# A hybrid two-layer encoder on one core: a reordered beginning, routing and end, and experts of 64 slots in one stationary operand

## The chip, the cores and the metric

The kernel runs on one core of a Trainium2 chip. The metric is the device time of one execution in microseconds (us). Five engines work side by side, each through its own list of instructions in order: TensorE (PE, matmuls), VectorE (DVE), ScalarE (ACT), GpSimd (POOL) and SyncE (SP, which here issues the transfers). Semaphores make one wait for another.

## What is computed

256 tokens of width 1024 pass two layers. Each layer takes a modulated norm of x, a mixer (gated linear attention, differential attention and gated delta net, merged by gates), a residual, a second modulated norm, a feed-forward part and a residual. The feed-forward part of layer 0 is dense (width 2816), that of layer 1 is a mixture of eight experts of width 3584, of which each token takes the best two:

```python
mod = jnp.einsum('bd,lde->lbe', jax.nn.silu(c), adaln_w) + adaln_b[:, None, :]
for layer in range(DEPTH):
    sh1, sc1, g1, sh2, sc2, g2 = jnp.split(mod[layer][:, None, :], 6, axis=-1)
    h = rmsnorm(x, norm_w[layer, 0]) * (1.0 + sc1) + sh1
    y = hybrid_mixer(h, ...)
    x = x + g1 * rmsnorm(y, norm_w[layer, 1])
    h = rmsnorm(x, norm_w[layer, 2]) * (1.0 + sc2) + sh2
    y = swiglu(h, ...) if layer % 2 == 0 else moe_swiglu(h, ...)
    x = x + g2 * rmsnorm(y, norm_w[layer, 3])
def swiglu(h, w1, w3, w2):
    return (jax.nn.silu(h @ w1) * (h @ w3)) @ w2
def moe_swiglu(h, router_w, w1, w3, w2):
    top_val, top_idx = lax.top_k(t @ router_w, TOP_K)
    combine = einsum(softmax(top_val), one_hot(top_idx, N_EXPERTS))
    for e in range(N_EXPERTS):
        out = out + combine[:, e:e + 1] * swiglu(t, w1[e], w3[e], w2[e])
```

## The kernel before

All weights are fp32 and are read once, in tiles of 128x1024 (two blocks of 128 input rows by 512 columns, 512 KB). For every tile SP starts a DMA into a ring of `raw` slots (line 286); ACT casts its high part `wh` (L319); DVE subtracts it from the tile and keeps the low part `wl` (L320, the *split* below). An activation is held in the same way as a high and a low part, and PE makes three products: high by high, high by low, low by high. The tiles come in a planned order: `load_ahead` issues transfers, `take` gives the next split tile, and casts and splits are issued some four tiles ahead of the matmuls that use them. `Side` and `pump` weave smaller work (a generator that yields how many steps it wants to wait) between the tiles; inside `by_hand` the order of the program is the order of each engine.

The stages, by time in the profile: the beginning (to 55 us), mixer 0 (to about 350), the dense ffn (to 545), mixer 1 (to 870), routing (to 895), the experts (to 1840) and the end.

*Beginning.* `begin` loads x and sixteen `rawe` tiles of adaln_w for shift and scale. `sums` accumulates each tile either on PE (L509, against the column `scol`) or on DVE (L450, L452) into `acc`, which `end` then sums over partitions on PE. The first eight tiles give columns 0 to 511 of the modulation, and with them the first half of the projection `gv` (`mm_nat`, L400 to L403) runs; the late eight tiles give the other half. `gates_small` (L841) multiplies a small tile of w_in (`small`, L831 to L833), and `proj_T("nk")` (L439) follows.

*Transitions.* `transition` interleaves the residual `r` (squares L724, `yg` = y times the gain row L730, `rr` = the reciprocal root L692 and L693, `up` L737) with the next norm `n` (squares L639, `xn` L648, transposes `tr` L660, modulated columns `hf` L668 and L670, their high part `hi` L674 and low part `lo` L678) for token blocks 0 and 1. `down_proj` is the matmul group before it.

*Experts.* Routing sorts the experts by their count. The five biggest get 128 slots (*full*), the last three get 64 (*half*); a run-time branch at the end repeats the work with 128 slots for all if a half expert had more than 64 tokens. `gather` picks an expert's tokens by matmuls with one-hot matrices (L1884), eight blocks for the high part and eight for the low part, casts them to `gx` (L1887), and transposes the one-hots to `hT` (L1899). It runs for groups of experts (0), (1), (2, 3), (4, 5), (6, 7), each from block 4 of the expert before on. An expert has seven blocks of 512 hidden columns. A block takes four tiles of w1, four of w3 and, of the block before, four of w2. The up-projection is L1991 to L1993 (1 of 128 rows `gH`, `gL` each times a 128x512 piece). `gated` makes silu (ACT, L2001) and the multiply (DVE, L2002) at 128x512. `turned` transposes the product on PE (L1946) and keeps high and low part (`aTm`). `down` multiplies it (L1913, L1914 for half experts, L1916 to L1918 for full ones).

In a half expert, the one-hot stands twice side by side: rows 0 to 63 and rows 64 to 127 of the gathered tile are the same 64 tokens. The two halves of the transposed tile then hold the high and the low part of the same tokens, so that `down` needs two matmuls in place of three. The up-projection makes three with the tokens doubled.

After an expert's last block, `parted` keeps `ywH` and `ywL` (L1925, L1926) and `scatter` (L1938 to L1940) adds it to `acc` with the routing weight. `finish` applies the last residual.

## Time and profile before

| | us |
|---|---|
| median of three runs (1858.14 to 1862.54) | 1859.29 |
| the profiled execution | 1858.87 |
| its span, first to last instruction | 1857.0 |
| PE busy in the span | 1817.3 (98%) |
| DVE busy | 1591.7 (86%) |
| ACT busy | 1319.6 (71%) |
| POOL busy | 28.2 (2%) |
| DMA, mean over the span | 286 GB/s, 531 MB |

The busy times of engines overlap. PE is nearly always busy, so the chain that ended last is 73% PE; by its lines the three up-projection matmuls of the experts have 11% of the span each. DVE's largest group is L320 (893 splits, 1066.6 us), ACT's is L319 (893 casts, 927.5 us). The share over the whole span is a mean over stages, so the rows below go by stages.

### The profile page before, as it was taken

What the parts mean: (1) busy time and instruction counts of PE and PEld (TensorE: products, weight loads), DVE (VectorE), ACT (ScalarE), POOL (GpSimd) and SP (SyncE); (2) the same over time, 40 slices, a digit from 0 to 9 for tenths busy, and PEclk for the clock granted to TensorE, in tenths of its full rate; (3) what the DMA queues carried; (4) which work ended last, traced back from release to release, by engine and by line L of the source; (5) the groups of instructions that cost most, each with busy time, mean ns of one, the idle gap of its engine ahead of it and who ended that gap; (6) DMA issues with size and microseconds to landing.
All of it is one profiled execution on the core that took longest, in us unless ns stands there. A gap on an engine that the chain in (4) does not pass through costs nothing.

```text
span 1857.0 us, 33213 instructions
## 1 busy us (share of the span) xinstructions
PE 1817.3 (98%) x11988; PEld 1534.8 (83%) x11988; DVE 1591.7 (86%) x2034; ACT 1319.6 (71%) x1872; POOL 28.2 (2%) x54
## 2 busy tenths in 40 slices
PE   7999999999999999999999999999999999999997
PEld 6987888799978978888788888888888888878785
DVE  6887986788856888867898998999989999999998
ACT  3786476644456774774788788787787778888885
POOL 0000000000000000000000000000000000000000
PEclk9999999999999999999999999999999999999998
DMA  9545765699764547669899999999999999999993
GB/s 323 164 145 149 238 193 184 204 311 302 237 210 126 148 149 229 204 201 328 289 350 318 358 347 348 360 377 356 369 349 359 378 366 383 393 382 393 393 393 141
DMA packets 258027, 531.35 MB, mean 286 GB/s; under 512 B 22126, under 2 KB 45116, under 8 KB 257852
## 3 DMA queue, kind: packets, MB, share of 16 engines
q1 hardware_dynamic: 257500, 528.99, 82.0%
q8 instruction: 96, 1.57, 0.4%
q14 instruction: 79, 0.65, 0.1%
q0 software_dynamic: 192, 0.07, 0.0%
q10 hardware_dynamic: 160, 0.07, 0.0%
HBM read 528.02 MB, written 1.05 MB: 285 GB/s over the span
## 4 chain that ended last, share of the span: by engine, by line
PE 73%; DVE 3%; DMA 2%; ACT 1%; issue 1%; POOL 0%; DVEq 0%; ACTq 0%
PE mo L1992 11%; PE mo L1991 11%; PE mo L1993 11%; PE my L1916 3%; PE my L1917 3%; PE my L1918 3%; PE pt L439 3%; PE pt L440 3%; PE pt L441 3%; PE pn L400 3%; PE pn L403 3%; PE pn L401 2%; DVE wl L320 2%; PE my L1914 2%; PE my L1913 2%; PE maT L1946 1%
## 5 line engine op out<-in xcount | busy, mean ns | idle before, releaser
L320 DVE TENSOR_TENSOR wl<-raw,wh 128x1024 fp32r<-128x1024 f32 (+1 forms) x893 | 1066.6, 1220 | 142.4 <-ACT wh L319 112.9
L319 ACT CAST wh<-raw 128x1024 fp32r<-128x1024 f32 (+1 forms) x893 | 927.5, 1054 | 319.1 <-PE mo L1993 79.5
L1991 PE MATMUL mo<-wh,gx 128*128 128x512 f32 x896 | 355.7, 397 | 0.1
L1992 PE MATMUL mo<-wl,gx 128*128 128x512 f32 x896 | 350.4, 391 | 2.0 <-DVE wl L320 1.9
L1993 PE MATMUL mo<-wh,gx 128*128 128x512 f32 x896 | 349.8, 390 | 0.0
L1992 PEld LDWEIGHTS mo<-wl,gx 128*128 128x128 f32 x896 | 168.6, 188 | 38.8 <-DVE wl L320 5.6
L1993 PEld LDWEIGHTS mo<-wh,gx 128*128 128x128 f32 x896 | 168.2, 188 | 35.7 <-ACT gx L1887 0.4
L1991 PEld LDWEIGHTS mo<-wh,gx 128*128 128x128 f32 x896 | 168.4, 188 | 32.7 <-ACT gx L1887 0.5
L439 PE MATMUL pt<-xH,wh 128*128 128x256 f32 x576 | 166.4, 289 | 0.0
L440 PE MATMUL pt<-xH,wl 128*128 128x256 f32 x576 | 163.7, 284 | 0.0
L441 PE MATMUL pt<-xL,wh 128*128 128x256 f32 x576 | 163.6, 284 | 0.0
L400 PE MATMUL pn<-wh,xH 128*128 128x512 f32 x352 | 148.2, 421 | 0.0
L403 PE MATMUL pn<-wh,xL 128*128 128x512 f32 x352 | 138.1, 392 | 0.0
L401 PE MATMUL pn<-wl,xH 128*128 128x512 f32 x352 | 137.9, 392 | 0.2 <-issue 0.2
L440 PEld LDWEIGHTS pt<-xH,wl 128*128 128x128 f32 x576 | 111.3, 193 | 0.2
L439 PEld LDWEIGHTS pt<-xH,wh 128*128 128x128 f32 x576 | 111.2, 193 | 0.3
L441 PEld LDWEIGHTS pt<-xL,wh 128*128 128x128 f32 x576 | 111.2, 193 | 0.0
L1916 PE MATMUL my<-wh,aTm 128*128 128x512 f32 x280 | 109.1, 390 | 0.0
L1917 PE MATMUL my<-wl,aTm 128*128 128x512 f32 x280 | 109.0, 389 | 0.0
L1918 PE MATMUL my<-wh,aTm 128*128 128x512 f32 x280 | 108.9, 389 | 0.0
L400 PEld LDWEIGHTS pn<-wh,xH 128*128 128x128 f32 x352 | 66.2, 188 | 18.6 <-issue 7.4
L403 PEld LDWEIGHTS pn<-wh,xL 128*128 128x128 f32 x352 | 66.1, 188 | 14.8
(476 smaller groups left out, 2639.2 us busy)
## 6 DMA issues: line engine op xcount, KB each, us to landing
raw<-in_moe_w SPq DMA_DIRECT2D x672, 512.0 KB, 5.8
raw<-in_w_in SPq DMA_DIRECT2D x128, 512.0 KB, 4.0
raw<-in_ffn_w SPq DMA_DIRECT2D x66, 512.0 KB, 5.0
raw<-in_adaln_w SPq DMA_DIRECT2D x48, 512.0 KB, 4.1
rawa<-in_adaln_w SPq DMA_DIRECT2D x32, 512.0 KB, 6.3
raw<-in_w_branch SPq DMA_DIRECT2D x24, 512.0 KB, 4.7
rawe<-in_adaln_w SPq DMA_DIRECT2D x16, 512.0 KB, 7.9
raw<-in_w_out SPq DMA_DIRECT2D x16, 512.0 KB, 4.7
```

The costliest lines, as they stand in the source:

```text
L319: S.copy(H, r)
L320: low = lambda: tt(L, r, H, op=OP.subtract)
L400: mm(o, xH[:, tb, k, :], H, start=k == 0, stop=False)
L401: mm(o, xH[:, tb, k, :], L, start=False, stop=False)
L403: mm(o, xL[:, tb, k, :], H, start=False, stop=k == last)
L439: mm(d, H[:, cs], xH[:, :, k, :], start=k == 0 and c % 2 == 0, stop=False, skip_group_check=True)
L440: mm(d, L[:, cs], xH[:, :, k, :], start=False, stop=False, skip_group_check=True)
L441: mm(d, H[:, cs], xL[:, :, k, :], start=False, stop=k == KD - 1, skip_group_check=True)
L1916: mm(y[hf], aT[:, 0, k, :], H[:, c], start=first, stop=False)
L1991: mm(q, gH[:, k, :], H, start=k == 0, stop=False)
L1992: mm(q, gH[:, k, :], L, start=False, stop=False)
L1993: mm(q, gL[:, k, :], H, start=False, stop=k == KD - 1)
```

## The change

1. *Beginning.* The order of x, rows and adaln tiles in SP's queue changes; the `small` tile is loaded behind the last gv tiles and all of its matmuls come later; the late tiles that PE sums are numbers 4 and 5 instead of 0; `product` runs per token block; constants (`other_loads`) load later; two matmuls `keep_warm` stand around the first sums' end.
2. *Transitions and routing.* The second token block's squares come before the multiplies by the gain row; in `down_proj`'s last tiles block 1 makes its left half first; in routing, transposes take the place of warm matmuls.
3. *Half experts.* The tokens are gathered once, 64 wide, and one `gx` tile holds their high part in columns 0 to 63 and their low part in 64 to 127. The up-projection then makes two matmuls for three. Its result has two halves of partitions that must be added. `gated` only copies both results from PSUM (two ACT copies). `turned`, now after the second w1 tile of the next block, multiplies each 128x128 piece by `fold`, two identities of 64 on top of each other, which transposes and adds; then silu on ACT and multiply on DVE at 128x256, and the high (ACT) and low part (DVE) of the product. The one-hots are doubled by POOL (`twice`) for `hT`. Groups of the gather: (0), (1), (2, 3), (4), (5, 6, 7).
4. *End.* Token block 0's two multiplies `yg` run on POOL, ahead of the reciprocal roots, and block 1's come before the stores.

```diff
+    def keep_warm():
+
+        mm(ps("warm", [P, 512], "pw"), ident, x[:, 0, 0:512], start=True, stop=True)
+
@@ -542,12 +546,15 @@
             s0.add(v, k0, load(v, 0, k0), i in (1, 3))
             part(i)
         load_ahead([None] * 2)
-        order = [(1, 0), (1, 2), (1, 4), (1, 6), (0, 0), (0, 2), (0, 4), (0, 6)]
-        late = [load(v, 1, k0) for v, k0 in order[:2]]
-        load_ahead([None, None, "l4"])
-        late += [load(v, 1, k0) for v, k0 in order[2:]]
+        order = [(v, k0) for v in (1, 0) for k0 in range(0, KD, 2)]
+        late = [load(v, 1, k0) for v, k0 in order[:3]]
+        load_ahead([None] * 2)
+        late += [load(v, 1, k0) for v, k0 in order[3:]]
+        late = [(v, k0, r, i in (4, 5)) for i, ((v, k0), r) in enumerate(zip(order, late))]
         lows = []
+        keep_warm()
         s0.end()
+        keep_warm()
         issue_one()
         issue_one(lows)
         s0.bias()
@@ -562,33 +569,32 @@
         load_ahead([None] * 2)
         o = [ps("pn", [P, 512], "pw") for _ in range(2)]
-        def product(early, tb, i):
-            for k, H, L in early:
-                mm_nat(o[tb], k, H, L, xs, tb, KD - 1, (i,))
+        def product(early, tb):
+            for i in range(2):
+                for k, H, L in early:
+                    mm_nat(o[tb], k, H, L, xs, tb, KD - 1, (i,))
         s1 = sums(1)
-        late = [(v, k0, r, i == 0) for i, ((v, k0), r) in enumerate(zip(order, late))]
+        early = [p for _ in range(2) for p in take("gv", False)]
+        product(early, 0)
         s1.add(*late[0])
-        early = [p for _ in range(2) for p in take("gv", False)]
-        for tb in range(2):
-            for i in range(2):
-                product(early, tb, i)
+        s1.add(*late[1])
         issue_one()
-        s1.add(*late[1])
-        small = take("small", False)
-        osm = gates_small(xs, small[:4])
-        issue_one()
-        load_ahead([None] * 2)
-        other_loads()
+        product(early, 1)
         s1.add(*late[2])
-        issue_one()
+        issue_one(lows)
+        lows.pop()()
+        load_ahead([None])
         s1.add(*late[3])
-        s1.end(1)
         n.tr(0, 1, ("pg",))
         n.tr(1, 1, ("pl",))
+        s1.add(*late[4])
+        s1.add(*late[5])
+        s1.add(*late[6])
         onk = proj_T("nk", 512, xs, rows=2)
-        for i in range(4, 8):
-            s1.add(*late[i])
+        other_loads()
+        s1.end(1)
+        s1.add(*late[7])
         issue_one(lows)
...
         n.tr(0, 0)
         n.tr(0, 1)
         warm(fill)
+        r.sq(1, 0)
         r.yg(1, 0, grow)
-        r.sq(1, 0)
         then()
-        r.yg(1, 1, grow)
         r.sq(1, 1)
         r.rs(1)
+        r.yg(1, 1, grow)
...
         def by_block(n, between):
             ps_ = [p for _ in range(n) for p in take(name, False)]
             for tb in range(2):
-                for k, H, L in ps_:
-                    for hf in range(2):
-                        add_(k, H, L, tb, hf)
+                todo = [(p, hf) for p in ps_ for hf in range(2)]
+                for (k, H, L), hf in sorted(todo, key=lambda t: t[1]) if tb else todo:
+                    add_(k, H, L, tb, hf)
                 if between and tb == 0:
                     between()
@@ -1864,27 +1865,34 @@
                 slots, m, comb, half = tl("slb", [P, 2, NE], "gs"), m01, combk, ()
                 tt(slots, slot, first_slot[:, None, :].to_broadcast([P, 2, NE]), op=OP.subtract)
             nb = DE // 512
-            groups = deque(((0,), (1,), (2, 3), (4, 5), (6, 7)))
+            groups = deque(((0,), (1,), (2, 3), (4,), (5, 6, 7)) if half else ((0,), (1,), (2, 3), (4, 5), (6, 7)))
+            if half:
+
+                fold = abT[:, 0:64]
+                tt(fold, ident[:, 0:64], ident[:, 64:128], op=OP.add)
             def gather(es, every):
                 hot = hots.pop(0) if hots else one_hot(slots, m, es, half)
                 if es[0]:
-                    yield 16
-                n = len(es)
-                gs = [[tl("gx", [P, KD, P], "e4", F32R) for _ in range(2)] for _ in es]
+                    yield 10 if es[0] in half else 16
+                n, small = len(es), es[0] in half
+                width = 64 if small else P
+
+                gs = [[tl("gx", [P, KD, P], "e4", F32R) for _ in range(1 if small else 2)] for _ in es]
                 hT = [tl("hT", [P, 2, P], "l1", F32R) for _ in es]
                 for j, e in enumerate(es):
                     of[e] = gs[j], hT[j]
                 for k in range(0, KD, 2):
                     for part, src in enumerate((hH, hL)):
-                        o = ps("gx", [P, 2, n, P])
+                        o = ps("gx", [P, 2, n, width])
                         for i in range(2):
                             for tb in range(2):
                                 mm(o[:, i], src[:, tb, (k + i) * P:(k + i) * P + P], hot[tb],
                                    start=tb == 0, stop=tb == 1)
                         for j in range(n):
-                            S.copy(gs[j][part][:, k:k + 2, :], o[:, :, j, :])
+                            g = gs[j][0][:, :, part * 64:part * 64 + 64] if small else gs[j][part]
+                            S.copy(g[:, k:k + 2, :], o[:, :, j, :])
                         if part == 0:
                             yield every
                     yield every
-                o = ps("hTp", [P, n, 2, P])
+                twice = tl("twice", [P, 2, P], "l1") if small else None
                 for j, e in enumerate(es):
+                    if small:
+
+                        for tb in range(2):
+                            G.tensor_copy(twice[:, tb, :].rearrange("p (i s) -> p i s", i=2),
+                                          hot[tb][:, j, None, :].bitcast(F32).to_broadcast([P, 2, 64]))
+                        yield 2
+                    o = ps("hTp", [P, 2, P])
                     for tb in range(2):
-                        nc.tensor.transpose(o[:, j, tb, :], hot[tb][:, j, :].bitcast(F32), ident)
-                for j in range(n):
-                    S.copy(hT[j], o[:, j])
+                        nc.tensor.transpose(o[:, tb, :], twice[:, tb, :] if small else hot[tb][:, j, :].bitcast(F32), ident)
+                    S.copy(hT[j], o)
+                    if j < n - 1:
+                        yield 1
@@ -1941,14 +1957,22 @@
             def turned(e, t):
+
+                if e in half:
+                    q = ps("maT", [P, 2, 4, 64])
+                    for i in range(2):
+                        for k in range(4):
+                            mm(q[:, i, k, :], t[i][:, k * P:k * P + P], fold, start=True, stop=True)
+                    a = tl("ma", [P, 4, 64], "m2")
+                    act(a, q[:, 0], AF.Silu)
+                    tt(a, a, q[:, 1], op=OP.mult)
+                    aT = tl("aTm", [P, 4, P], "m4", F32R)
+                    S.copy(aT[:, :, 0:64], a)
+                    tt(aT[:, :, 64:128], a, aT[:, :, 0:64], op=OP.subtract)
+                    return aT
                 q = ps("maT", [P, 4, P])
                 for k in range(4):
                     nc.tensor.transpose(q[:, k, :], t[:, k * P:k * P + P], ident)
-                if e in half:
-                    aT = tl("aTm", [P, 4, P], "m4", F32R)
-                    S.copy(aT[:, :, 0:64], q[:, :, 0:64])
-                    tt(aT[:, :, 64:128], q[:, :, 64:128], aT[:, :, 0:64], op=OP.subtract)
-                    return aT
@@ -1986,20 +2010,28 @@
                                 next(first)
                                 if k0 == KD - 2:
                                     Side(first, 8)
-                            gH, gL = of[e][0]
+                            g, gL = of[e][0][0], of[e][0][-1]
                             for k, H, L in take(w, not (final and w == "moe_w3" and k0 >= KD - 4)):
-                                mm(q, gH[:, k, :], H, start=k == 0, stop=False)
-                                mm(q, gH[:, k, :], L, start=False, stop=False)
-                                mm(q, gL[:, k, :], H, start=False, stop=k == KD - 1)
+                                mm(q, g[:, k, :], H, start=k == 0, stop=False)
+                                mm(q, g[:, k, :], L, start=False, stop=e in half and k == KD - 1)
+                                if e not in half:
+                                    mm(q, gL[:, k, :], H, start=False, stop=k == KD - 1)
                                 pump()
+                            if prev is not None and w == "moe_w1" and k0 == (2 if prev[0] in half else KD - 2):
+                                aT = turned(prev[0], prev[2])
                         o.append(q)
-                        if prev is not None and w == "moe_w1":
-                            aT = turned(prev[0], prev[2])
-                    t = tl("ma", [P, 512], "m2")
+                    if e in half:
+                        t = [tl("ma", [P, 512], "m2") for _ in range(2)]
+                    else:
+                        t = tl("ma", [P, 512], "m2")
                     def gated():
-                        act(t, o[0], AF.Silu)
-                        tt(t, t, o[1], op=OP.mult)
+                        if e in half:
+                            S.copy(t[0], o[0])
+                            S.copy(t[1], o[1])
+                        else:
+                            act(t, o[0], AF.Silu)
+                            tt(t, t, o[1], op=OP.mult)
...
@@ -2022,14 +2054,14 @@
             for tb in range(2):
                 r.sq(tb, 0)
                 r.sq(tb, 1)
+            r.yg(0, 0, grow, G)
+            r.yg(0, 1, grow, G)
             r.rs(0)
-            r.yg(0, 0, grow)
-            r.yg(0, 1, grow)
+            r.yg(1, 0, grow)
+            r.yg(1, 1, grow)
             r.rs(1)
             r.store(0, 0)
             r.store(0, 1)
-            r.yg(1, 0, grow)
-            r.yg(1, 1, grow)
             r.store(1, 0)
             r.store(1, 1)
```

The places where an order of instructions matters most, as built. First DVE in a plain block of a half expert: `wl` is a split, `ma` the gated product, `maT` its transpose in PSUM, `aTm` the high and low part. Before:

```order
L320 TENSOR_TENSOR wl_17391<-raw_17388,wh_17390 128x1024
L2002 TENSOR_TENSOR ma_17351<-ma_17351,mo_17292 128x512
L320 TENSOR_TENSOR wl_17404<-raw_17401,wh_17403 128x1024
L320 TENSOR_TENSOR wl_17416<-raw_17413,wh_17415 128x1024
L320 TENSOR_TENSOR wl_17428<-raw_17425,wh_17427 128x1024
L320 TENSOR_TENSOR wl_17440<-raw_17437,wh_17439 128x1024
L1950 TENSOR_TENSOR aTm_17454<-maT_17449,aTm_17454 128x4x64
L320 TENSOR_TENSOR wl_17461<-raw_17458,wh_17460 128x1024
```

and of the change:

```order
L320 TENSOR_TENSOR wl_17326<-raw_17323,wh_17325 128x1024
L320 TENSOR_TENSOR wl_17339<-raw_17336,wh_17338 128x1024
L320 TENSOR_TENSOR wl_17349<-raw_17346,wh_17348 128x1024
L1968 TENSOR_TENSOR ma_17365<-ma_17365,maT_17356 128x256
L1971 TENSOR_TENSOR aTm_17368<-ma_17365,aTm_17368 128x4x64
L320 TENSOR_TENSOR wl_17374<-raw_17371,wh_17373 128x1024
```

The multiply moved from behind the block's last matmuls to directly ahead of the subtraction, with no split between the two.

ACT at the same place (`wh` is a cast of a weight tile). Before:

```order
L2001 ACTIVATE ma_17351<-mo_17237 128x512
L319 CAST wh_17403<-raw_17401 128x1024
L319 CAST wh_17415<-raw_17413 128x1024
L319 CAST wh_17427<-raw_17425 128x1024
L319 CAST wh_17439<-raw_17437 128x1024
L1949 CAST aTm_17454<-maT_17449 128x4x64
L319 CAST wh_17460<-raw_17458 128x1024
```

and of the change:

```order
L2030 COPY ma_17285<-mo_17180 128x512
L2031 COPY ma_17286<-mo_17234 128x512
L319 CAST wh_17338<-raw_17336 128x1024
L319 CAST wh_17348<-raw_17346 128x1024
L1967 ACTIVATE ma_17365<-maT_17356 128x256
L1970 CAST aTm_17368<-ma_17365 128x4x64
L319 CAST wh_17373<-raw_17371 128x1024
```

The cast L1970 reads what DVE's L1968 writes, and the cast of the next weight tile (`wh_17373`) stands behind it; DVE's next split (`wl_17374`) reads that one.

DVE between mixer 0 and the ffn, token block 1 of the residual and block 0 of the next norm (`hf`). Before:

```order
L730 TENSOR_TENSOR yg_4077<-po_3940,grow_3851 128x512
L668 TENSOR_SCALAR hf_4062<-xT_4063,ncol_4034,modT 128x128 x2
L730 TENSOR_TENSOR yg_4077<-po_3944,grow_3851 128x512
L692 TENSOR_SCALAR rr_4090<-rss_4079 128x1
L668 TENSOR_SCALAR hf_4062<-xT_4069,ncol_4034,modT 128x128 x2
```

and of the change:

```order
L735 TENSOR_TENSOR yg_4090<-po_3950,grow_3861 128x512
L673 TENSOR_SCALAR hf_4072<-xT_4073,ncol_4044,modT 128x128 x2
L697 TENSOR_SCALAR rr_4099<-rss_4087 128x1
L735 TENSOR_TENSOR yg_4090<-po_3960,grow_3861 128x512
L673 TENSOR_SCALAR hf_4072<-xT_4079,ncol_4044,modT 128x128 x2
```

The second multiply moved behind the reciprocal root, directly ahead of the columns of the second `hf`.

## Rows read from the trace of the kernel before

**Rows 1.** Busy time by stretch; busy us (x instructions), granted clock, DMA share, GB/s.

```profile
911.60:1518.00 606.40, 606.40 (x2792) 503.37 (x2791) 562.10 (x556) 487.21 (x547) 1.92 (x2) 1.00 0.99 356
1518.00:1830.00 312.00, 309.96 (x1414) 253.62 (x1414) 302.88 (x299) 262.98 (x303) 0.00 (x0) 1.00 1.01 381
1660.00:1800.00 140.00, 139.03 (x629) 114.00 (x628) 137.76 (x135) 118.00 (x130) 0.00 (x0) 1.00 1.04 393
```

**Rows 2.** Groups of lines in 1518 to 1830 us: busy us, mean ns | idle before.

```profile
L320 DVE TENSOR_TENSOR wl<-raw,wh 128x1024 fp32r<-128x1024 f32 x237 | 276.9, 1217 | 9.3 <-ACT wh L319 3.0 <-PE my L1913 1.5 <-DMA raw<-in_moe_w 0.5
L319 ACT CAST wh<-raw 128x1024 fp32r<-128x1024 f32 x236 | 240.9, 1053 | 31.1 <-PE mo L1993 27.1 <-DVE ma L2002 0.9 <-DVE wl L320 0.3
...
L1946 PE MATMUL maT<-cc,ma 128*128 128x128 f32 x80 | 12.0, 272 | 0.0
...
L1940 DVE SCALAR_TENSOR_TENSOR acc<-sc,cvT,acc 128x512 f32<-128x512 f32 x12 | 8.9, 740 | 0.0
```

**Rows 3.** Timeline of DVE, a plain half block: start us, us, instruction.

```profile
1667.33 0.68 DVE L2002 TENSOR_TENSOR ma<-ma,mo 128x512 f32<-128x512 f32 x1
1667.93 4.62 DVE L320 TENSOR_TENSOR wl<-raw,wh 128x1024 fp32r<-128x1024 f32 x4
1672.47 0.42 DVE L1950 TENSOR_TENSOR aTm<-maT,aTm 128x256 fp32r<-128x256 f32 x1
1672.80 9.62 DVE L320 TENSOR_TENSOR wl<-raw,wh 128x1024 fp32r<-128x1024 f32 x8
1682.34 0.68 DVE L2002 TENSOR_TENSOR ma<-ma,mo 128x512 f32<-128x512 f32 x1
```

**Rows 4.** Timeline of PE, first and last of 21 successive matmuls.

```profile
1820.41 0.39 PE L1993 MATMUL mo<-wh,gx 128*128 128x512 f32 x1
...
1824.95 0.39 PE L1992 MATMUL mo<-wl,gx 128*128 128x512 f32 x1
```

**Rows 5.** Timeline of ACT, the same half block.

```profile
1671.21 0.37 ACT L1949 CAST aTm<-maT 128x256 fp32r<-128x256 f32 x1 [0.75 <-PE maT L1946]
...
1676.71 3.90 ACT L319 CAST wh<-raw 128x1024 fp32r<-128x1024 f32 x4 [0.30 <-PE mo L1993]
```

**Rows 6.** Timeline of DVE, gated multiplies around the gather of experts 6 and 7.

```profile
1568.85 0.68 DVE L2002 TENSOR_TENSOR ma<-ma,mo 128x512 f32<-128x512 f32 x1
...
1618.97 0.68 DVE L2002 TENSOR_TENSOR ma<-ma,mo 128x512 f32<-128x512 f32 x1
```

**Rows 7.** Timeline of ACT, silus around the gather of 4 and 5, and plain.

```profile
1328.11 0.59 ACT L2001 ACTIVATE ma<-mo 128x512 f32<-128x512 f32 x1
...
1382.94 0.59 ACT L2001 ACTIVATE ma<-mo 128x512 f32<-128x512 f32 x1
...
1435.19 0.58 ACT L2001 ACTIVATE ma<-mo 128x512 f32<-128x512 f32 x1
...
1452.01 0.59 ACT L2001 ACTIVATE ma<-mo 128x512 f32<-128x512 f32 x1
```

**Rows 8.** Timeline of DVE, ACT and PE in the beginning.

```profile
37.71 5.48 DVE L452 SCALAR_TENSOR_TENSOR acc<-rawe,scol,acc 128x512 f32<-128x512 f32 x7
...
43.79 1.05 ACT L319 CAST we<-raw 128x1024 fp32r<-128x1024 f32 x1 [0.31 <-DMA raw<-in_w_in]
...
48.60 0.40 PE L400 MATMUL pn<-we,xH 128*128 128x512 f32 x1
```

**Rows 9.** Timeline of DVE and ACT, from mixer 0 to the ffn.

```profile
359.29 0.68 DVE L730 TENSOR_TENSOR yg<-po,grow 128x512 f32<-128x512 f32 x1
361.40 0.21 DVE L692 TENSOR_SCALAR rr<-rss 128x1 f32<-128x1 f32 x1 [1.43 <-ACT rsq L724]
361.54 0.72 DVE L668 TENSOR_SCALAR hf<-xT,ncol,modT 128x128 f32<-128x128 f32 x2
...
358.75 0.60 ACT L724 ACTIVATE rsq<-po 128x512 f32<-128x512 f32 x1 [0.46 <-DVE yg L730]
```

**Rows 10.** Groups of lines of POOL: busy us, mean ns | idle before.

```profile
L1013 POOL COPY Yc<-cc 128x256 f32<-128x256 f32 x4 | 2.9, 715 | 115.0 <-PE q L1052 82.7 <-DMA cc<-in_consts 32.3
```

More of the change, by code (lines that the diff above doesn't have):

```diff
@@ L607, in begin @@
         for tb in range(2):
-            for i in range(2):
-                product(early, tb, i)
-        return o, osm, small[4:], onk
+            product(early, tb)
+        return o, None, None, onk
     def row_of(col, name):
@@ L1368, in plan_mixer @@
             first = [plan.popleft() for _ in range(7)]
-            plan.extendleft(reversed([first[i] for i in (0, 1, 4, 5, 6, 2, 3)]))
+            plan.extendleft(reversed([first[i] for i in (0, 1, 5, 6, 2, 3, 4)]))
     def mixer(l, xs, o, more, then=(), begun=(None, None, None)):
@@ L1703, in one_hot @@
         def one_hot(slots, m, es, half):
[L1705 removed]
+            n = 64 if es[0] in half else P
+            hot = [tl("hot", [P, len(es), n], "l1", F32R) for _ in range(2)]
             for tb in range(2):
                 for j, e in enumerate(es):
[L1708 to L1712 removed]
+                    ts(hot[tb][:, j, :], C("iota")[:, 0:n], slots[:, tb, e:e + 1], m[:, tb, e:e + 1],
+                       op0=OP.is_equal, op1=OP.mult)
             return hot
@@ L1728, in moe @@
             logits(0, 1)
-            warm(1)
+            nat(0, 0)
             n.rs(1)
```

35 lines of the change are left out of this document (15 added, 20 removed).

## The prediction

> **What bounds the kernel now.** I read the busy time by stretch first. From 911.6 to 1518 us, where full experts (128 slots) run, PE is busy for all of 606.40 us while DVE has 562.10. From 1518 to 1830, where experts of 64 slots run, PE has 309.96 of 312.00 us, but DVE 302.88 and DMA 381 GB/s, and 393 GB/s between 1660 and 1800 [rows 1]. So PE is the bound in both, with a second and a third engine 3% behind it in the half stage. The groups of that stage say what DVE does: 237 splits (the low part of a weight tile) are 276.9 of its 302.9 us, and it idles 9.3 us before them [rows 2]. The timeline of one plain block shows the beat: 12 splits, one multiply (0.68 us) and one subtraction of the turned tile (0.42), and 15.01 us from a multiply to the next, 1667.33 to 1682.34. Four splits in a row take 4.62 us, each 1.217 long, so they start (4.62 - 1.22)/3 = 1.133 us apart; the eight after the turned tile take 9.62, so 1.20 apart [rows 3], because ACT's casts wait for PE (27.1 us of waits on L1993) [rows 2]. DVE's own pace is therefore 1.133 a tile, 13.6 us a block; it is held back to 15.0 by PE.
>
> **Experts of 64 slots, steady blocks.** PE loses a third of its up-projection matmuls: 16 of 48 a block. From 1820.41 to 1824.95 there are 20 starts, 4.54 us in all [rows 4], so 0.227 us each: 16 x 0.227 = 3.6 us a block less. Its four fp32 transposes, 272 ns each [rows 2], become eight fp32 matmuls of 64 columns, about as much again. So PE would need about 12 us of the old 15.0, and it stops being the bound.
>
> What takes over is in the order of the instructions. Before, the turned tile needs one cast on ACT and one subtraction on DVE, and ACT's next casts need nothing of DVE. Now ACT runs silu, then a cast of the *product*, and only then the next weight cast; DVE runs the multiply, then a subtraction that needs ACT's cast, then the next split, which needs ACT's weight cast. That is a round trip DVE, ACT, DVE in which neither engine has other work to put first. Its price: multiply 128x256 from PSUM 0.42 (the row of the old subtraction of that shape, [rows 3]); cast of 128x256, 0.37 long, of which the next cast overlaps 0.10 (four of 1.053 take 3.90), so 0.27; that weight cast 1.05 [rows 2, 5]; three hand-overs between engines at 0.08 in all (an estimate; no row isolates one, 0 to 0.3). 0.42 + 0.27 + 1.05 + 0.08 = 1.82 us in which DVE does 0.76 us of work. The other 12 splits stay at 1.133 us: 12 x 1.133 + 1.82 = 15.42 us a block instead of 15.00, **+0.42 us in 20 blocks, +8.4 us**. The lower bound is no stall at all (DVE's work alone, 13.6 + 0.42 + 0.34 = 14.36: -12.8 us over 20 blocks, which DMA limits, see the second rival); the upper bound adds lateness of silu, if the eight fp32 matmuls take twice 0.27 us each (4.3 us), which is past the 3.4 us of three splits that stand between the tile they follow and the multiply: +1 us a block, +20. I take the sum, since every term has a row of its own shape and only the hand-overs are estimated.
>
> The two copies of `gated` add 2 x 0.59 - 0.59 to ACT, and the silu shrinks. ACT has 240.9 us of casts in 312 [rows 2] and 13.6 us a block to run 12 casts at 0.97 (3.90 for four, [rows 5]) and these: hidden; without that cover 0.6 a block. The subtraction L1971 is hidden behind ACT's weight cast.
>
> **Scatter of a finished expert.** It now costs PE-bound blocks 1667.33 - 1618.97 - 45.0 = 3.4 us [rows 3, 6]. On DVE it is 4 accumulations of 0.74 [rows 2] and 2 subtractions of 128x512, at the 0.68 of the multiply of that shape [rows 3], 4.3 us, which will be seen whole where DVE is the bound: +0.9, for three experts; part of it falls into ACT's round trip: **+1.5** (0 to +2.4).
>
> **Gather.** The group of experts 6 and 7 costs 1618.97 - 1568.85 - 45.0 = 5.1 us in the half stage [rows 6]. It goes. The group of experts 4 and 5 costs 1382.94 - 1328.11 - 3 x 16.82 = 4.4 us in full blocks (16.82 between the silus at 1435.19 and 1452.01) [rows 7]; it becomes one expert of half the columns, the same 32 matmuls: -0.5 for the two transposes and the shorter rows. The new group of 5, 6 and 7 has 32 matmuls of 192 columns and 6 transposes, in full blocks, where PE is the bound: between one expert's and two experts' price, +4.6. Its six POOL copies of 128x128 hold up nobody if each takes no more than the 0.72 us of a 128x256 POOL copy [rows 10]. Sum **-1.0** (-2 to +1).
>
> **Begin.** PE's second half of the gv projection starts at 48.60, after the modulation columns: DVE accumulates to 43.19, and the last gv tile is cast from 43.79 [rows 8]. Now four of eight late tiles are summed on PE or earlier, and the small-gate load is behind the gv tiles. So DVE's chain and the gv landing both end some 3 to 4 us earlier, but 12 of the gate matmuls of 256 columns (at half of 0.227, 1.4 us) move from a gap of PE into its dense part, and 16 scaled columns more stand in PE's queue ahead of nk. SP's loads of constants now stand in front of three w_in tiles. **-1.6** (-3.5 if all of the earlier landing shows, +1.5 if nk's third tile becomes the late one). The two `keep_warm` matmuls lie in a wait for DMA: 0.
>
> **Transitions.** The square of the second token block no longer waits 0.46 us for DVE's multiply, but the multiply of its second half (0.68), which ran in DVE's gap at 359.29, now stands between rr (361.40) and hf (361.54) [rows 9]. Net +0.68 - 0.46 = +0.2, twice: **+0.5** with the tail of down_proj (-0.9 to +1.4). Late next is xH. Routing swaps a warm matmul for real work: **-0.3** (-0.8 to +0.3).
>
> **End.** Two of four yg multiplies go to POOL, beside the POOL's two powers; on DVE one takes 0.68 [rows 9]. If POOL takes DVE's time for them, they run beside the squares and one pair goes off the path (-1.1 with what is left of the wait for rr); POOL's 128x256 copy is 0.72 [rows 10], so 512 columns 1.43 and the pair 2.9, of which the squares of the same block, two at 0.6 [rows 9], cover 1.3: the power behind them is 1.6 late (+1.6). I take **-0.4**.
> The Trainium skill, "GPSIMD Engine Reference", section 3.1 (Elementwise), gives 4497 ns on GpSimd against 2293 on VectorE for an fp32 tensor_tensor of 2048 elements and says to use the vector engine. An estimate from that page for 512 elements is 1.1 us each; by it the pair would hold the powers back about 2.2 us and the end would come out near +0.5, so it speaks against this edit. No run here has shown a POOL multiply of that size.
>
> **Sum.** +8.4 + 1.5 - 1.0 - 1.6 + 0.5 - 0.3 - 0.4 = +7.1, on the profiled execution of 1858.87 us: **1866.0 us**. The median of the three runs is 1859.29, 0.4 above the profiled one, so this is +0.36% of it. About 0.3%, 5.6 us, is what a measurement of this kernel tells from no change, so the forecast lies hardly beyond that line.
>
> **Rivals.**
> *The round trip is small or the smaller edits pay more* (same). For it: ACT may have the next weight cast under way by other means of the order than I read, and Begin can give 3.5. Half the round trip's excess and Begin at its best give 7.1 - 4.2 - 1.9 = +1.0: 1860. Against it: the order stands. Chance 0.30.
> *DMA sets the pace* (faster). If DVE finds its splits ready, it needs 14.36 us a block, and 12 tiles of 0.524 MB at 393 GB/s take 16.0. The bytes of the half stage, 381 x 312, would take 302.5 us at 393 [rows 1]: -9.5; with the other parts -1.8: 1858.87 - 11.3 = 1847.6. This decides once the round trip is under about 0.9 us a block. Against it: each of its terms is a row. Chance 0.14.
> The Trainium skill, "DMA: Bandwidth & Descriptors", section Specifications, gives about 358 GB/s from HBM per core. By it a block of 6.29 MB could not take less than 17.6 us and the change could gain nothing. The trace disagrees: 393 GB/s over 140 us.
> *Silu comes late, or the clock drops* (much slower). PE would idle 3 us in 15. The granted clock is 1.00 in all the stretches I read [rows 1], but PE is 99% busy in them; none shows what a PE at 80% is granted. Lateness of +0.5 us a block gives 20 x 0.5 more, 1876. Chance 0.06.
> *The edit does not do what it says*: were the fall-back branch taken (an expert over 64 slots), the half path would not run; before, it runs. Chance under 0.01.
>
> **How the numbers follow.** Forecast 0.49, same 0.30, DMA 0.14, much slower 0.06. The forecast's own spread, 1861 to 1872, puts a fifth of it within 0.3% and hardly any below; the same-rival lends a little to faster. So faster 0.16, same 0.36, slower 0.48. The range leaves out the DMA rival's lower half and the much slower case: 1850 to 1873.
>
> **What would show it.** Right: PE busy under 85% between 1518 and 1835, with DVE named as what its matmuls wait for; blocks of 15.3 to 15.5 us from multiply to multiply, with DVE idle 0.9 to 1.1 us before the split after L1968 and L1971, ended by ACT; no gather rows there; the last gv product 2 to 4 us earlier. Wrong: plain blocks of 15.0 or less, or DVE waiting for DMA of in_moe_w in the half stage.

## The result, and the profile after

The changed kernel takes 1871.04 us (median of four executions, 1868.41 to 1873.76) against 1859.97 for the kernel before (four, 1858.14 to 1862.54): a ratio of 1.0062, interval 1.0046 to 1.0077. It is slower by 0.6%, 11 us. The profiled execution took 1868.41 us, its span is 1866.6 us, 9.6 more than before. It was the fastest of the four; their mean granted clocks are 0.997, 0.992, 0.992 and 0.990 for 1868.41, 1870.68, 1871.39 and 1873.76 us.

Busy time by stretch of the changed kernel, columns as in [rows 1]:

```profile
911.60:1518.00 606.40, 605.88 (x2807) 502.32 (x2806) 559.89 (x559) 488.78 (x563) 5.92 (x8) 1.00 0.98 353
1518.00:1830.00 312.00, 292.80 (x1279) 203.44 (x1277) 292.53 (x290) 263.32 (x319) 0.00 (x0) 1.00 1.03 385
1660.00:1800.00 140.00, 131.76 (x566) 89.84 (x565) 131.47 (x130) 120.18 (x144) 0.00 (x0) 1.00 1.04 392
```

Against [rows 1], PE's work in the half stage fell from 1414 to 1279 matmuls, and DVE's from 302.88 to 292.53 us: neither is full any more. DMA still moves 385 GB/s. The groups of the stretch say where the time went (busy us, mean ns | idle before):

```profile
L320 DVE TENSOR_TENSOR wl<-raw,wh 128x1024 fp32r<-128x1024 f32 x234 | 268.8, 1217 | 10.5 <-ACT wh L319 10.2
...
L2016 PE MATMUL mo<-wl,gx 128*128 128x512 f32 x307 | 130.2, 424 | 14.6 <-DVE wl L320 14.6
...
L1965 PE MATMUL maT<-abT,ma 128*128 128x64 f32 x304 | 36.0, 271 | 0.0
...
L1971 DVE TENSOR_TENSOR aTm<-ma,aTm 128x256 fp32r<-128x256 f32 x19 | 8.1, 425 | 9.0 <-ACT aTm L1970 9.0
...
L1970 ACT CAST aTm<-ma 128x256 fp32r<-128x256 f32 x19 | 7.7, 407 | 14.7 <-DVE ma L1968 14.7
L1967 ACT ACTIVATE ma<-maT 128x256 f32<-128x256 f32 x19 | 7.3, 385 | 25.3 <-PE maT L1965 25.3
```

DVE's idle time is ahead of two kinds of instruction, both released by ACT: 10.2 us before splits, waiting for ACT's weight cast, and 9.0 us before the subtraction L1971, waiting for ACT's cast of the product. ACT in turn idles 14.7 us before that cast, for DVE's multiply, and 25.3 before silu, for the fold. PE waits for DVE's splits (14.6 us on L2016), where before ACT's casts waited for PE [rows 2]. The timeline of DVE and then of ACT over one plain block shows the chain itself:

```profile
1674.55 0.41 DVE L1968 TENSOR_TENSOR ma<-ma,maT 128x256 f32<-128x256 f32 x1
1675.43 0.42 DVE L1971 TENSOR_TENSOR aTm<-ma,aTm 128x256 fp32r<-128x256 f32 x1 [0.47 <-ACT aTm L1970]
1676.38 13.71 DVE L320 TENSOR_TENSOR wl<-raw,wh 128x1024 fp32r<-128x1024 f32 x12 [0.53 <-ACT wh L319]
1690.02 0.41 DVE L1968 TENSOR_TENSOR ma<-ma,maT 128x256 f32<-128x256 f32 x1
...
1674.02 0.39 ACT L1967 ACTIVATE ma<-maT 128x256 f32<-128x256 f32 x1 [1.48 <-PE maT L1965]
1674.99 0.41 ACT L1970 CAST aTm<-ma 128x256 fp32r<-128x256 f32 x1 [0.58 <-DVE ma L1968]
1675.30 9.87 ACT L319 CAST wh<-raw 128x1024 fp32r<-128x1024 f32 x10
```

From a multiply to the next it is 15.47 us, 15.01 in [rows 3]. The twelve splits now follow each other without a gap (13.71 us, so 1.136 apart), but before them DVE idles 0.47 and 0.53 us. The gather of experts 5, 6 and 7 stretches three full blocks as foretold; the multiplies of DVE around it:

```profile
1455.34 0.68 DVE L2034 TENSOR_TENSOR ma<-ma,mo 128x512 f32<-128x512 f32 x1
...
1510.30 0.68 DVE L2034 TENSOR_TENSOR ma<-ma,mo 128x512 f32<-128x512 f32 x1
```

54.96 us for three blocks of 16.82: 4.5 us [rows 7]. By landmarks (start of an instruction of PE, before and after) the 9.6 us come together so:

| up to | before | after | change in this stretch |
|---|---|---|---|
| end of the gate matmuls (L224) | 55.61 | 53.17 | -2.4 |
| first matmul of the ffn (L1574, L1579) | 360.84 | 363.23 | +4.8 |
| first up-projection matmul of the experts | 895.8 | 898.3 | +0.1 |
| last up-projection matmul | 1831.1 | 1839.5 | +5.9 |
| last scatter matmul | 1843.7 | 1854.5 | +2.4 |
| end of the span | 1857.0 | 1866.6 | -1.2 |

The round trip adds 0.46 us in each of 19 blocks (+8.7), scatter adds 1.7 in all, and the gathers give back 1.0 (4 alone -0.4; 5, 6 and 7 +4.5; 6 and 7 gone, -5.1). That makes +9.5, and the table has +5.9, because blocks of their own kind take 3.6 back. The first half block is 2.2 us shorter: it has 16 matmuls less and no round trip yet. Its first matmul and that of the next block, before and then after (16.81 and 14.57 us):

```profile
1502.61 0.39 PE L1991 MATMUL mo<-wh,gx 128*128 128x512 f32 x1
...
1519.42 0.39 PE L1991 MATMUL mo<-wh,gx 128*128 128x512 f32 x1
...
1509.23 0.39 PE L2015 MATMUL mo<-wh,gx 128*128 128x512 f32 x1
...
1523.80 0.39 PE L2015 MATMUL mo<-wh,gx 128*128 128x512 f32 x1
```

The row of gains `grow`, made on PE near the end (1800.7 us before, 1809.1 after), lengthened the two blocks around it by 1.4 us before (31.4 against 30.0) and by 0.4 now (31.4 against 30.9), and the last block is 0.4 shorter up to its last up-projection matmul. The 4.8 us between 55 and 361 were nowhere in the forecast: 3.2 of them come between 334 and 361 us (see down_proj_only below) and 1.4 between 191 and 212, whose cause no run isolates. Nor were the 2.4 us behind the last up-projection matmul. The -2.4 at the gate matmuls is for the most part not the change's (see three_steps_begin below).

### The profile page after: what moved, and what is told of

Its sections match the earlier page's. It is cut to its first block, busy times and chain, and to the rows that moved or that the text cites. A ratio compares the mean times of both kernels' runs of the same rounds, so it can differ in the third digit from the quotient of the medians.

```text
span 1866.6 us, 33145 instructions
## 1 busy us (share of the span) xinstructions
PE 1809.1 (97%) x11922; PEld 1488.9 (80%) x11922; DVE 1581.9 (85%) x2031; ACT 1325.5 (71%) x1914; POOL 34.9 (2%) x62
## 4 chain that ended last, share of the span: by engine, by line
PE 73%; DVE 4%; ACT 1%; issue 1%; DMA 0%; POOL 0%; ACTq 0%; DVEq 0%
PE mo L2016 11%; PE mo L2015 10%; PE mo L2018 7%; PE my L1932 3%; PE my L1933 3%; PE my L1934 3%; PE pn L400 3%; PE pn L403 3%; PE pt L439 3%; PE pt L441 3%; PE pt L440 3%; PE pn L401 3%; PE my L1930 2%; DVE wl L320 2%; PE maT L1965 2%; PE my L1929 2%
## 5 line engine op out<-in xcount | busy, mean ns | idle before, releaser
L319 ACT CAST wh<-raw 128x1024 fp32r<-128x1024 f32 (+1 forms) x893 | 917.8, 1052 | 290.3 <-PE pn L403 81.8
L2016 PE MATMUL mo<-wl,gx 128*128 128x512 f32 x896 | 360.7, 403 | 15.7 <-DVE wl L320 15.7
L2015 PE MATMUL mo<-wh,gx 128*128 128x512 f32 x896 | 357.7, 399 | 2.0 <-ACT wh L319 1.9
L2016 PEld LDWEIGHTS mo<-wl,gx 128*128 128x128 f32 x896 | 168.4, 188 | 81.5 <-DVE wl L320 52.1
L2018 PE MATMUL mo<-wh,gx 128*128 128x512 f32 x560 | 218.7, 391 | 0.0
L2015 PEld LDWEIGHTS mo<-wh,gx 128*128 128x128 f32 x896 | 168.5, 188 | 32.9 <-ACT wh L319 3.5
L2018 PEld LDWEIGHTS mo<-wh,gx 128*128 128x128 f32 x560 | 105.2, 188 | 23.1 <-ACT gx L1895 0.5
L403 PEld LDWEIGHTS pn<-wh,xL 128*128 128x128 f32 x352 | 66.1, 188 | 14.7
```

Source lines behind the costliest of these rows:

```text
L319: S.copy(H, r)
L403: mm(o, xL[:, tb, k, :], H, start=False, stop=k == last)
L2015: mm(q, g[:, k, :], H, start=k == 0, stop=False)
L2016: mm(q, g[:, k, :], L, start=False, stop=e in half and k == KD - 1)
L2018: mm(q, gL[:, k, :], H, start=False, stop=k == KD - 1)
```

## The experiments

Ten kernels ran, in three sets, each set on one chip beside runs of the kernel before (medians 1858.80 of 29 executions, 1858.75 of 23 and 1858.38 of 23). The theory: in each block of a half expert DVE and ACT wait for each other in turn, and this is the loss. The rival: the half experts gain as PE's relief suggests, and the stages ahead of them lose.

**half_only**, part 3 of the change alone:

```diff
-groups = deque(((0,), (1,), (2, 3), (4, 5), (6, 7)))
+groups = deque(((0,), (1,), (2, 3), (4,), (5, 6, 7)) if half else ((0,), (1,), (2, 3), (4, 5), (6, 7)))
...
+                if e in half:
+                    q = ps("maT", [P, 2, 4, 64])
...
+                        if e in half:
+                            S.copy(t[0], o[0])
+                            S.copy(t[1], o[1])
```

> The kernel before with the half experts' part of the change alone (gather groups, one stationary operand, fold, doubled one-hots). Theory (the round trip DVE, ACT, DVE in every block of a half expert is the cost): the whole of the loss is here; from the first expert matmul to the last scatter the changed kernel lost 8.3 us (2.5 behind at 896, 10.8 behind at the last scatter), so about 8 us slower than before, near 1868, blocks of 15.47 us. Rival (the loss comes from the reordered stages ahead of the experts, the half experts gain): at or below 1857.

Measured: 1867.52 us, ratio 1.0042 (1.0029 to 1.0055), +8.7. The theory holds: most of the loss is here, and the size is that expected. In its profile the stretch from the first up-projection matmul to the last scatter matmul (898.87 to 1855.05) takes 956.2 us, as it does in the changed kernel (898.32 to 1854.50), against 947.9 before: +8.3.

**no_half**, the changed kernel without part 3 (the first pair of lines stands for it), and **no_half_no_down**, that with the old down_proj as well (the rest). Its expectation speaks of the old transition too, but the kernel that ran keeps the new one:

```diff
-groups = deque(((0,), (1,), (2, 3), (4,), (5, 6, 7)) if half else ((0,), (1,), (2, 3), (4, 5), (6, 7)))
+groups = deque(((0,), (1,), (2, 3), (4, 5), (6, 7)))
...
-todo = [(p, hf) for p in ps_ for hf in range(2)]
-for (k, H, L), hf in sorted(todo, key=lambda t: t[1]) if tb else todo:
-    add_(k, H, L, tb, hf)
+for k, H, L in ps_:
+    for hf in range(2):
+        add_(k, H, L, tb, hf)
```

> The change without its half experts' part: beginning, transitions, down_proj, routing and end alone. Theory: 2.5 us behind at the first expert matmul, 1.2 won back at the end: about 1 us slower than before, 1860 to 1861, within noise. Rival (as above): about 1867 or more.

> As no_half, also with the old order of down_proj and the old transition. Theory: the new order of down_proj's last tiles let a weight tile of the ffn be cast ahead of one of w_out at 342 us; PE waited 2.2 us there and ran 3.4 us at half the clock. Without it: no such waits, some 3 us less than no_half, about 2 us faster than before, 1857 to 1858. Rival (the late w_out tile comes from the beginning, whose tiles arrive in another rhythm): as no_half, 1860 to 1861, with the wait at 343 still there.

Measured: 1864.16 us (1.0027, 1.0017 to 1.0037), +5.4; and 1860.65 us (1.0007, 0.9999 to 1.0016), +1.9. The two kernels differ by down_proj's order alone, so the 3.5 us between them (some 2.4 either way by the two intervals) are its price, near the 3 us foretold; both stand 3 to 4 us above what the landmarks of one profile had promised. The mean granted clock over the twelve executions of each was 0.9924 and 0.9931, that of the kernel before 0.9957: 0.003 of 1860 us is about 5 us (an estimate from these clocks). The landmarks had come from an execution at 0.997. So much of what these two kernels lost is clock, and why it was lower no run isolates.

**two_steps**, the test of the theory on the changed kernel: the cast and the subtraction of the product go one weight tile later.

```diff
-    S.copy(aT[:, :, 0:64], a)
-    tt(aT[:, :, 64:128], a, aT[:, :, 0:64], op=OP.subtract)
-    return aT
+    return a if later else kept(a)
...
+if prev is not None and w == "moe_w1" and k0 == 4 and prev[0] in half:
+    aT = kept(aT)
```

> The changed kernel with one edit: the high and low part of the product are made one weight tile later than silu and multiply, so that a cast and a split stand between them. Theory (round trip): DVE's stall of about 1.0 us a block goes, blocks of 14.4 to 14.6 us where weights are there, then 16.0 where DMA at 393 GB/s sets the pace; DMA saturated from about 1520, last tile some 3 us earlier than before: 1847 to 1853, faster than before by 7 to 12. Rival 1 (the blocks are longer because PE, idle a fifth of the time, is slower, or silu is late): blocks stay near 15.4, 1868 to 1872. Rival 2 (DVE's own work fills the block, no stall to take away): 1865 to 1870.

Measured: 1859.11 us (0.9995, 0.9984 to 1.0005): 12 us less than the changed kernel's median, though not yet faster than before. Its DVE in a plain block, and ACT's silu there:

```profile
1767.77 0.41 DVE L1974 TENSOR_TENSOR ma<-ma,maT 128x256 f32<-128x256 f32 x1
1768.58 1.23 DVE L320 TENSOR_TENSOR wl<-raw,wh 128x1024 fp32r<-128x1024 f32 x1 [0.40 <-ACT wh L319]
1769.72 0.42 DVE L1961 TENSOR_TENSOR aTm<-ma,aTm 128x256 fp32r<-128x256 f32 x1
...
1782.55 0.41 DVE L1974 TENSOR_TENSOR ma<-ma,maT 128x256 f32<-128x256 f32 x1
...
1782.01 0.39 ACT L1973 ACTIVATE ma<-maT 128x256 f32<-128x256 f32 x1 [1.46 <-PE maT L1971]
1782.29 1.04 ACT L319 CAST wh<-raw 128x1024 fp32r<-128x1024 f32 x1
```

The block is 14.78 us. Both stalls of the round trip are gone, and a smaller one of 0.40 stands ahead of the split behind the multiply: its weight cast stands behind silu, which had waited 1.46 us for the fold. So rival 1 (slow PE) and rival 2 (no stall) fall; the time was 6 us above the expected 1847 to 1853, and this wait of 0.40 in 20 blocks makes 8. The changed kernel had also been profiled in an execution at a granted clock of 0.997; these twelve had 0.992 in the mean.

**three_steps**, the kernel before with parts 3 and 4, fold, then silu and multiply, then high and low part, each a weight tile after the other; **three_steps_begin** has part 1 as well:

```diff
+if prev[0] in half:
+    if k0:
+        aT = (folded, product, kept)[k0 // 2 - 1](aT if k0 > 2 else prev[2])
+elif k0 == KD - 2:
+    aT = turned(prev[0], prev[2])
...
+return {1: first, 2: second}
```

> The kernel before with the change's half experts and end; fold, silu with multiply, and high with low part each one weight tile after the other (in the last block the last two likewise). Theory: two_steps kept a stall of 0.40 us a block, as its weight cast stands behind a silu that waits for the fold; now no wait is left and a block is 12 x 1.133 + 0.41 + 0.34 = 14.35 us, until DMA (16.0 a block) has used up the tiles that lie ready: 1848 to 1853, faster than before by 6 to 11. Rival (DMA or PE sets a pace near that of two_steps): blocks of 14.8, 1853 to 1858.

> three_steps with the change's beginning as well. If the beginning is worth the 2.2 us that the profile of the changed kernel shows at 103 us: 2 us less than three_steps. Rival (the 2.2 us depend on the clock and on when tiles land; the profiles of four kernels with this beginning stood between 1.7 ahead and 2.2 behind at that place): within 1 us of three_steps.

Measured: 1851.35 us (0.9954, 0.9941 to 0.9967), 7.4 us less than the kernel before, 20 less than the changed one and 16 less than half_only, from which it differs only in the order of these steps and in part 4; and 1850.93 us (0.9957, 0.9944 to 0.9970). DVE in a plain block of three_steps:

```profile
1692.48 0.41 DVE L1965 TENSOR_TENSOR ma<-ma,maT 128x256 f32<-128x256 f32 x1
1692.81 1.22 DVE L320 TENSOR_TENSOR wl<-raw,wh 128x1024 fp32r<-128x1024 f32 x1
1693.94 0.42 DVE L1971 TENSOR_TENSOR aTm<-ma,aTm 128x256 fp32r<-128x256 f32 x1
1694.32 12.58 DVE L320 TENSOR_TENSOR wl<-raw,wh 128x1024 fp32r<-128x1024 f32 x11
1706.82 0.41 DVE L1965 TENSOR_TENSOR ma<-ma,maT 128x256 f32<-128x256 f32 x1
```

14.34 us from multiply to multiply, the 14.35 of the sum, and no idle time of DVE left. Nearer the end the next limit shows: among the waits between 1518 and 1835 us (us in total, times, longest) there is one for DMA:

```profile
DVE wl L320 <- ACT wh L319: 5.4, 9, 0.8
...
ACT wh L319 <- DMA raw<-in_moe_w: 4.0, 14, 0.5
```

ACT waits 14 times for tiles to land, which the lists of the changed kernel and of two_steps do not have. As for the beginning, the two kernels differ by 0.4 us, with five executions each and ranges that overlap (1849.13 to 1852.15 and 1850.23 to 1853.01): its gain of 2.4 us in one profile is not there in the times. The clock explains that profile. The same stretch in the kernel before and in the changed one, columns as in [rows 1]:

```profile
40.00:60.00 20.00, 18.94 (x123) 17.42 (x122) 15.53 (x49) 12.30 (x25) 1.06 (x2) 0.91 0.78 247
40.00:60.00 20.00, 20.00 (x147) 18.69 (x146) 13.26 (x46) 12.00 (x28) 2.77 (x6) 1.00 0.69 214
```

The kernel before had been profiled in an execution with 0.91 here. Four kernels with the old beginning show 1.00 from 20 to 60 us (routing_only, down_proj_only, transition_only, three_steps), and their gate matmuls end at 53.73 to 54.39 us; the two with the new one and 1.00 (the changed kernel, no_half) at 53.17 and 53.70. So the beginning is worth about 0.6 us there, by six profiles, and 0.3 at the first matmul `kk` near 98 us. There the four kernels that had this beginning first stood 2.2, 1.7 and 0.1 us ahead of the kernel before and 1.2 behind, not 2.2 behind as the expectation has it. In three_steps_begin the granted clock was 0.96 in 20 to 40 us and 0.95 in 40 to 60, in two_steps 0.90 and 0.92, in no_half_no_down 0.78 and 0.96: the two `keep_warm` matmuls, which all three have, did not keep it up in these executions.

**routing_only**, **down_proj_only**, **end_only** and **transition_only**, one small edit each on the kernel before:

```diff
-warm(1)
+nat(0, 0)
...
+for (k, H, L), hf in sorted(todo, key=lambda t: t[1]) if tb else todo:
...
+r.yg(0, 0, grow, G)
+r.yg(0, 1, grow, G)
...
+r.sq(1, 0)
 r.yg(1, 0, grow)
```

> The kernel before with the change's routing alone. Theory: with the warm matmuls gone PE waits uncovered between 880 and 900 us, and the clock falls there to half in some executions (three of four profiles with this routing show a granted clock of 0.75 to 0.91 in 880 to 900 or 900 to 920, none without it does): +0.5 to +2 us. Rival (the row in the changed kernel's own profile, which gains 0.7 there): -0.7.

> The kernel before with the change's order of down_proj's last tiles alone. Theory: this edit alone makes the scheduler put the cast of a ffn tile ahead of that of a w_out tile, as the order of ACT shows; PE waits about 2 us near 343 and the clock may fall behind it: +2 to +3.5 us, 1861 to 1862.5. Rival (it is the transition's new order that costs): within 1 us of before.

> The kernel before with the change's end alone (two multiplies on POOL). Theory: from the first square to the end of the last store 6.5 us in the profile of two_steps against 7.4 before, although POOL needs 1.26 us a piece: 1 us less, too small for the times, to be read from that stretch. Rival (POOL slows the DVE multiplies beside it, and the powers come late): the stretch is as long as before or longer.

> The kernel before with the transition's new order alone (squares ahead of multiplies). By the prediction's term: +0.2 a transition, between the first xn and the first matmul of the next stage, lost in the noise: within 1 us of before. Rival (it is this edit that makes no_half slower than the sum of its parts): +2 us or more.

Measured: 1859.12 us (1.0001, 0.9992 to 1.0011); 1861.43 (1.0010, 0.9999 to 1.0022); 1858.52 (1.0002, 0.9991 to 1.0013); 1860.34 (1.0005, 0.9994 to 1.0016). Each interval contains 1; the medians are +0.4, +2.7, +0.1 and +2.0. For routing both stories stay open: its profile shows the fall of the clock that was foretold (0.83 in 880 to 900 us), but so does that of three_steps_begin, which keeps the old routing (0.91). The other three can be read in their profiles. In down_proj_only, ACT at w_out (a `we` of the ffn now stands ahead of two `wh`, the first of them of w_out), and what PE waits for there, in us in total, times, longest:

```profile
340.94 1.05 ACT L319 CAST we<-raw 128x1024 fp32r<-128x1024 f32 x1 [0.96 <-DMA raw<-in_ffn_w]
341.89 1.99 ACT L319 CAST wh<-raw 128x1024 fp32r<-128x1024 f32 x2
```

```profile
PE po L1533 <- ACT wh L319: 1.2, 1, 1.2
PE po L1534 <- DVE wl L320: 0.9, 1, 0.9
```

and its busy time by stretch (columns as in [rows 1]):

```profile
340.00:345.00 5.00, 2.81 (x12) 1.78 (x11) 4.21 (x4) 2.94 (x3) 0.00 (x0) 1.00 0.72 217
345.00:350.00 5.00, 5.00 (x16) 3.95 (x15) 2.16 (x3) 2.09 (x2) 0.00 (x0) 0.66 0.83 279
```

PE waits 2.1 us (before 0.6), and from 345 to 350 us its granted clock is 0.66, two thirds of the time at half speed (0.34 lost, at half speed 0.68 of the time). The edit named no cast; the order built from it has one cast in ACT's queue behind a cast that waits for DMA. It is no accident of one execution: from w_out's first matmul (`po`, 333.66 us before) to its first on a `we` tile (346.83) it takes 16.2 to 16.4 us in the four profiles with this order (down_proj_only, the changed kernel, no_half, two_steps), 13.2 in the kernel before and 12.9 to 13.0 in the seven others without it. In transition_only, DVE:

```profile
355.53 0.49 DVE L648 TENSOR_SCALAR xn<-x,nr 128x512 f32<-128x512 f32 x1 [0.59 <-POOL nr L693]
356.86 0.69 DVE L730 TENSOR_TENSOR yg<-po,grow 128x512 f32<-128x512 f32 x1 [0.84 <-ACT rsq L724]
357.47 0.72 DVE L668 TENSOR_SCALAR hf<-xT,ncol,modT 128x128 f32<-128x128 f32 x2
359.52 0.21 DVE L692 TENSOR_SCALAR rr<-rss 128x1 f32<-128x1 f32 x1 [1.33 <-ACT rsq L724]
359.65 0.68 DVE L730 TENSOR_TENSOR yg<-po,grow 128x512 f32<-128x512 f32 x1
360.25 0.72 DVE L668 TENSOR_SCALAR hf<-xT,ncol,modT 128x128 f32<-128x128 f32 x2
```

From xn to the second hf it is 4.72 us, 0.75 more than the 3.97 of the kernel before (357.57 to 361.54, the first here and the second in [rows 9]):

```profile
357.57 0.49 DVE L648 TENSOR_SCALAR xn<-x,nr 128x512 f32<-128x512 f32 x1 [0.59 <-POOL nr L693]
```

The multiply that ACT's square had waited for now waits 0.84 us for that square, and hf stands behind it. Of the 0.75 some 0.4 are left later in the ffn, where its transposes `gtT` start 23.33 us behind xn (at 378.86 us), 22.93 before (at 380.50). In end_only, DVE's last additions and POOL:

```profile
1842.67 1.62 DVE L730 TENSOR_TENSOR yg<-acc,grow 128x512 f32<-128x512 f32 x2
...
1844.34 2.72 DVE L741 SCALAR_TENSOR_TENSOR yg<-yg,rr,x 128x512 f32<-128x512 f32 x4
...
1840.62 2.52 POOL L730 TENSOR_TENSOR yg<-acc,grow 128x512 f32<-128x512 f32 x2 [882.29 <-issue]
1843.11 0.99 POOL L693 TENSOR_TENSOR rr<-rr,kon 128x1 f32<-128x1 f32 x1
```

From the first square (1840.49) to the end of the last addition (1847.06) are 6.6 us, 7.4 before (1842.76 to 1850.21): 0.9 us less, though POOL takes 1.26 us for a multiply of 128x512. That is read from one profile of each; the times (+0.1) do not show it.

## Why the prediction was right, and which of its steps were off

The direction, the mechanism and its place were right, and the measured 1871.04 us lies in the range of 1850 to 1873; the forecast of 1866.0 was 5 us short.

- *The round trip.* Put at 15.42 us a block, measured 15.47; the stall at 1.82 - 0.76 = 1.06, measured 0.47 + 0.53. From the multiply to the first split behind the subtraction it is 1.83 us (1674.55 to 1676.38) against 1.82, and the other splits take 13.64 against 13.60. The hand-overs at 0.08 were the one term that stood on no row; no run shows them alone, but the sum that they stand in came out. two_steps and three_steps show it to be the cause: with the same work and the wait taken out, 14.78 and 14.34.
- *Scatter and gather.* Scatter: 1624.32 to 1674.55 less three blocks of 15.47 is 3.82 against 3.36, so +0.5 for this one; the first costs +0.8, and the three together +1.7, foretold +1.5. Gather of 5, 6 and 7: foretold +4.6, measured 4.5.
- *The last block.* The step failed by leaving it out: "+0.42 us in 20 blocks" counts no 21st. It cost 2.4 us from the last up-projection matmul to the last scatter matmul: the fold takes 1.70 us where the transposes took 0.41, the way from it to the first matmul that reads the product takes 0.4 more, and the 16 matmuls from there on 0.6 more. The first half block, which has no round trip yet, was not singled out either, and gained 2.2.
- *Transitions.* "+0.68 - 0.46 = +0.2, twice" failed: taking ACT's wait of 0.46 for the multiply away gave DVE a wait of 0.84 for the square, which delays hf by 0.75, of which some 0.4 a transition last. And "the tail of down_proj" was taken as a detail; it moved a cast in ACT's queue at w_out and cost 2.7 us as a median. The profile of the changed kernel loses 3.2 us there. The forecast read the order of instructions at the edited lines, not elsewhere on the engines; the moved cast stood there.
- *Begin.* -1.6 was foretold, and -2.4 in the profile looks like more than that, but this is luck: the kernel before had been profiled at a granted clock of 0.91 in 40 to 60 us. Among profiles at 1.00 the gain is 0.3 to 0.6, and the times of three_steps_begin against three_steps have -0.4. The term was too large by about 1 us.
- *End.* -0.4 was foretold between -1.1 and +1.6; measured -0.9. The Trainium skill, "GPSIMD Engine Reference", section 3.1 (Elementwise), has 4497 ns for 2048 elements on GpSimd, 1.96 times VectorE's time. The prediction's estimate from it, 1.1 us, is near the 1.26 of the trace, and 1.26 over 0.68 is 1.85. What failed is the delay of the powers, put at 1.6 us. In end_only POOL's pair ends at 1843.14 and the power starts at 1843.11; DVE's reciprocal `rr`, which the power needs and which stands behind the last additions in DVE's queue, starts at 1842.55 and takes 0.20. So the power starts 0.36 us behind rr's end, 0.15 before (1845.02 to 1845.17): 0.2 late.
- *The DMA rival* was the state that the kernel reaches once the round trip is taken out: it was priced at 1847.6, and three_steps measured 1851.35 with ACT waiting for tiles. That it would need "the round trip under about 0.9 us a block" agrees with the runs: two_steps, where 0.40 of the stall is left, has no wait for DMA in its list.
- *The sign that PE would be busy under 85%* was wrong: it shows 292.80 of 312.00 us, 94%, with a third of the up-projection gone. A matmul's bar is 0.39 us long where 0.227 lies between starts, so short waits vanish in it; the mean bar of L2016 grew from 393 (L1992 before) to 424 ns instead. By starts PE needs less than 85%: the fold takes 1.70 us a block (1672.09 to 1673.79) where the four transposes took 0.36 (1508.05 to 1508.41 before), not about as much again as foretold, so 15.0 - 3.6 + 1.3 = 12.7 of 15.47 us, 82% (an estimate from these starts).
- *The sum.* That the forecast came within 5 us is in part luck. In the profiles it is +7.1 against +9.6. For the experts, from their first up-projection matmul to the last scatter matmul, 8.9 were foretold and 8.3 measured, with three parts in between that the forecast did not have (-2.2, -0.9 and +2.0) and that nearly cancel. Ahead of them the 4.8 us between 55 and 361 were missed, and the beginning's -2.4, mostly clock, hid half of them.

The sum of the single edits' medians, 8.7 + 2.7 + 2.0 + 0.4 + 0.1 - 0.4 = 13.5, is near the 11.1 of the whole; the parts under 3 us have intervals as wide as themselves, so it proves no more than their order.

## What to carry to other kernels

When a second and a third engine are nearly as full as the bound, taking work from the bound buys only the few per cent between them, and an operation that goes from DVE to ACT and back through queues in order costs both engines the whole trip, unless a piece of other work is put between its steps. Here the saving of a third of the matmuls lost 0.4% on its own, and with each step moved one weight tile later it won 0.5% (with the end's edit, which by itself made +0.1 us in the times). When a change is read by its order, the whole queue of each engine up to the next wait has to be compared, not only the edited lines.

## What the runs showed that was not expected

In end_only the pair of multiplies on DVE that took 1.28 us in the kernel before took 1.62, and 1.54 in the changed kernel. Its first 0.47 and 0.38 us lie beside the end of POOL's second multiply, and the 0.34 and 0.26 us lost are most of that time. POOL's power, which follows, did not cost it anything before: there the pair ran beside it (1845.17 to 1846.03 us) in 1.28. The additions L1940, which read one operand from PSUM, ran beside POOL's multiplies too and kept their 1.41 us a pair. What makes the two cases differ no run separates.

After PE's two waits of 1.2 and 0.9 us at w_out, the granted clock of down_proj_only was 0.66 in 345 to 350 us, so at the lower of its two levels (1.2 GHz) for two thirds of that time, although PE was busy in all of it. Such stretches came at changing places from one profile to another (0.91 in 40 to 60 us in the kernel before, 0.83 in 880 to 900 in routing_only, 0.75 in 900 to 920 in two_steps), so a difference of 2 us in a stage of this kernel says little from one profile alone; the 3 us at w_out could be told because eleven other profiles agree on which order has them.
